# A two-layer encoder with experts: order of the router's tail, splits ahead of the routing weights, norm roots by a power on POOL

## The chip, the cores and the metric

The kernel runs on one NeuronCore of a Trainium2 chip. The metric is the device time of one launch in microseconds (us). Engines are called PE (TensorE), DVE (VectorE), ACT (ScalarE), POOL (GpSimd) and SP (SyncE, which here only issues transfers).

## The reference

Two encoder layers work on 512 tokens of width 1024 in fp32. Cut to what matters here:

```python
for layer in range(2):
    h = rms_norm(x, norm1_g[layer])
    proj = h @ w_in[layer]                      # queries, keys, values of four mixers
    y_a, y_b, y_c, y_d = mla(...), dilated(...), gqa(...), diff(...)
    mixed = concat([rms_norm(y_a), rms_norm(y_b), rms_norm(y_c), y_d]) * mix_beta[layer]
    x = x + mixed @ w_out[layer]
    x = x + hier_moe(rms_norm(x, norm2_g[layer]), ...)

def hier_moe(t, wg, bg, we, be, w_gate, w_up, w_down):
    g_w, g_idx = top_k(softmax(t @ wg + bg), 1)          # one of 4 groups
    e_logits = (t @ we + be) of that group               # 4 experts each
    e_w, e_idx = top_k(softmax(e_logits), 2);  e_w /= sum(e_w)
    gate = one_hot(expert_id) * g_w * e_w                # 512 x 16
    for e in range(16):
        y += gate[:, e] * ((silu(t @ w_gate[e]) * (t @ w_up[e])) @ w_down[e])
```

`rms_norm` is `x * rsqrt(mean(x*x) + 1e-6) * gain`. Each expert has three fp32 matrices of 2 MB.

## The kernel before, in words

Tokens stand in four row tiles of 128 (index `t`). A layer is: norm and in-projection, the four mixers as 64 units of attention (head and row tile) in a software pipeline, out-projection and router in the last steps of that pipeline, then the 16 experts. An expert gets at most 96 tokens (`CAP`); what is beyond that would be done in rounds by `overflow()`, a `tc.If` on the number of rounds. With these inputs the branch isn't taken, but every engine loads the number (`nrd`) and branches there (L1461, L1470).

Every fp32 product is made from three: an operand is split into `hi` (a rounded copy, by ACT, L144) and `lo` (the difference, by DVE or POOL, L145), and `mm3` (L268) sums hi*hi, lo*hi and hi*lo. Weights are streamed in units of 128x1024 (512 KB) by the class `Weights`: a unit is loaded into a raw buffer by SP's queue, then split into one of six pairs of `hi` and `lo` buffers, and its raw buffer is free for the next load as soon as it is split. An expert has 12 units, four each of gate, up and down, each six matmuls on PE. The experts' order on PE is expert 0's gate and up, expert 1's gate, expert 0's down, expert 1's up, expert 2's gate, and so on.

The order of the work in the last steps of attention is a table, `TAIL`: the words of step 57 to 69 are run one after the other when that step of the pipeline has been issued. A letter is a function, a digit its row tile, and G or V (or none) the engine: `r` is the norm of the tile's new stream (`norm_x`, its root is the tile `r2`), `e` turns the tile, `f` makes the router's logits (`pl` on PE, `lg` on DVE), `h` the normed rows and their write to DRAM (`h2d`), `p` the ranks of the logits and the places of the tokens (`route`: `rank`, `M`, then `pp`, `pos`, `oh`), `x` picks expert 0's rows by a one-hot matmul (`acc`), `l` lists expert 1's rows (`pli`, L1141), `s` splits the next weight unit, `T` splits expert 0's turned rows (`xh`, `xl`), `K` makes the routing weights (`weights()`: some 25 small operations on DVE, among them the casts and subtractions of L1326 and L1328), `S` gathers expert 1's rows, `O` is the overflow. Engines run their instructions in the order in which they are issued, and a DMA issued by SP waits on SP for its buffer.

In the loop over experts a `todo` table says at which unit the one-hots of a later expert are made (`listed`, DVE, `oh` L341) and at which its list is made and its rows are gathered (`start`: PE `pli` L1381, POOL's gather L1393). Two units later its rows are turned (`ptg` L1405) and split.

A narrow norm takes its root by `rstd`: an integer first guess (three operations on DVE), then three Newton rounds, on DVE (nine operations) or on POOL (twelve).

Of the kernel before, what the change touches and what calls it, by code (L numbers as in the profile page):

```python
# [62 lines left out]
def hybrid_encoder(ctx: ExitStack, tc: tile.TileContext, I: dict, out: bass.AP, depth=2, dbg=None):  # L63
# [18 lines left out]
    tokb = cst.tile([128, NT, 2], BF, name="tokb")  # L82
    wlast = cst.tile([128, NT], FT, name="wlast")
    brep = drm.tile([8, 128, 1024], FT, name="brep")

    def late_constants():
# [33 lines left out]

    def rstd(pool, ss, n, inv, name, E=V):

        x = "" if E is V else "g"
        v = pool.tile([128, n], FT, name=name + "v", tag="rsv" + x, bufs=1)
        y = pool.tile([128, n], FT, name=name + "y", tag=name + "y")
        f = pool.tile([128, n], FT, name=name + "f", tag="rsf" + x, bufs=1)
        ti = pool.tile([128, n], I32, name=name + "i", tag="rsi" + x, bufs=1)
        V.tensor_scalar(v, ss, inv, EPS, op0=OP.mult, op1=OP.add)
        V.tensor_scalar(ti, v.bitcast(I32), 1, None, op0=OP.logical_shift_right)
        V.tensor_scalar(y.bitcast(I32), ti, -1, 0x5f3759df, op0=OP.mult, op1=OP.add)  # L130
        for _ in range(3):
            if E is V:
                V.scalar_tensor_tensor(f, v, -0.5, y, op0=OP.mult, op1=OP.mult)
                V.tensor_tensor(f, f, y, op=OP.mult)
                V.scalar_tensor_tensor(y, f, 1.5, y, op0=OP.add, op1=OP.mult)
            else:
                E.tensor_tensor(f, y, y, op=OP.mult)
                E.tensor_tensor(f, f, v, op=OP.mult)
                E.tensor_scalar(f, f, -0.5, 1.5, op0=OP.mult, op1=OP.add)
                E.tensor_tensor(y, y, f, op=OP.mult)  # L140
        return y
# [181 lines left out]
    for layer in range(depth):  # L323
# [32 lines left out]
        with ExitStack() as c2:  # L356
# [425 lines left out]
            with ExitStack() as c3:  # L782
# [134 lines left out]
                def finish(mi):  # L917
# [3 lines left out]
                    if mi == 2:  # L921
                        for t in range(NT):
                            sq = sm.tile([128, 512], FT, name="sq", bufs=1)
                            A.activation(sq[:, :256], y[:, t], AF.Square, accum_out=ss_[:, t:t + 1])
                        yield LATER
                        r = rstd(sm, ss_, NT, 1.0 / 256, "yr", G)
                        for t in range(NT):
                            if t in Y2G:
                                G.tensor_tensor(y[:, t], y[:, t], r[:, t:t + 1].to_broadcast([128, 256]), op=OP.mult)
                                G.tensor_tensor(y[:, t], y[:, t], late['beta'][:, sl], op=OP.mult)  # L930
                        yield LATER
                        for t in range(NT):
                            if t not in Y2G:
                                V.scalar_tensor_tensor(y[:, t], y[:, t], r[:, t:t + 1], late['beta'][:, sl],
                                                       op0=OP.mult, op1=OP.mult)
                        for _ in range(WAIT2):
                            yield LATER
                    else:
# [5 lines left out]
                        r = rstd(sm, ss_, NT, 1.0 / 256, "yr", G)  # L944
# [13 lines left out]
                def finish_pair():  # L958
# [30 lines left out]
                def norm_pair(t, E):  # L989
                    sl, y = slice(896, 1024), Y[3][:, t, 128:]  # L990
                    r = rstd(sm, late['yss', t], 2, 1.0 / 64, "yr", E)
                    if E is V:
# [17 lines left out]
                def norm_x(t, E):  # L1010
                    V.tensor_scalar(ss2[:, t, 0:1], ss2[:, t, 0:1], ss2[:, t, 1:2], None, op0=OP.add)
                    late['r', t] = rstd(sm, ss2[:, t, 0:1], 1, 1.0 / D, "r2", E)

# [43 lines left out]
                def logits(t):  # L1057
                    pl = ps.tile([128, 512], FT, name="pl", tag="tr")[:, :20]
                    for k in range(8):
                        PE.matmul(pl, late['xT'][t % 2][:, k], late['wr'][:, k], start=k == 0, stop=k == 7)  # L1060
                    V.scalar_tensor_tensor(lg[:, t], pl, late['r', t], late['brg'][:, :20], op0=OP.mult, op1=OP.add)

# [25 lines left out]
                def route(t):  # L1088


                    l4 = lg[:, t].rearrange("p (r e) -> p r e", e=4)
# [5 lines left out]
                    for k, op in enumerate((OP.is_gt, OP.is_ge)):  # L1097
# [5 lines left out]
                    V.scalar_tensor_tensor(M[:, t].rearrange("p (g e) -> p g e", g=4), rank[:, t, 4:].rearrange("p (g e) -> p g e", g=4),  # L1103
                                           2.0, goh[:, t, :, None].to_broadcast([128, 4, 4]), op0=OP.is_lt, op1=OP.mult)
                    pp = ps.tile([128, 512], FT, name="pp", tag="tr")
                    for u in range(t + 1):
                        PE.matmul(pp[:, :NE], tri[:, 0 if u == t else 1], M[:, u], start=u == 0, stop=u == t)
# [5 lines left out]
                    V.tensor_scalar(late['oh'][:, t], iota, pos[:, t, 0:1], None, op0=OP.is_equal)  # L1113
                    if t == NT - 1:
                        oh1 = scr[:, 1536:1536 + NT * CAP // 2].bitcast(BF).rearrange("p (t c) -> p t c", t=NT)
                        late['oh1'] = hots(1, oh1)
                        count_rounds(pp[:, NE:2 * NE])

# [27 lines left out]

                STAGES = dict(l=list_rows, b=norm_pair, c=turn_pair, o=open_out, d=close_out, e=turn_x, r=norm_x, f=logits, h=normed,
                              p=route, x=pick, s=lambda E: W.split(W.done + 1, E), w=warm)
# [151 lines left out]
        with ExitStack() as c2:  # L1300
# [157 lines left out]
            def overflow():  # L1458
# [11 lines left out]
                with tc.If(rounds > 1):  # L1470
                    V.memset(off, 0.0)
                    SP.dma_start(posd[0].rearrange("(t p) e -> p t e", p=128), pos)
                    SP.dma_start(posd[1].rearrange("(t p) e -> p t e", p=128), gate)
                    with tc.For_i(1, rounds):
                        V.tensor_scalar(off, off, float(CAP), None, op0=OP.add)
                        with tc.For_i(0, NE) as e:
                            one = bass.ds(e, 1)
                            pe_ = sm.tile([128, 2, NT], FT, name="pe")
                            for j in range(2):
                                SP.dma_start(pe_[:, j], posd[j, :, one].rearrange("(t p) o -> p (t o)", p=128))  # L1480
                            V.tensor_scalar(pe_[:, 0], pe_[:, 0], off, None, op0=OP.subtract)
# [190 lines left out]
```

## Time and profile before

| what | us |
|---|---|
| three runs | 1390.12, 1398.99, 1395.04 |
| their median | 1395.04 |
| the profiled execution | 1398.48 |
| its span, first to last instruction | 1396.6 |
| mean granted clock of TensorE | 0.966 of full speed |
| PE busy | 1296.7 (93%) |
| DVE busy | 1079.7 (77%) |
| ACT busy | 876.9 (63%) |
| POOL busy | 390.9 (28%) |

The profile is of one execution; all durations below come from it. Busy times are sums over the span and say nothing of when an engine stood still. A stage is read from windows (busy time of each engine in a stretch), then from the timeline of the engine that stands still there (each row with the idle time before it and the operation that ended that idle time), and then from the timelines of the engines named.

### The profile page before, as it was taken

The numbers are of one execution on the slowest core, as the hardware profiler recorded it, in microseconds if no ns is written. First come the engines' busy times: TensorE is split into PE (matmuls) and PEld (weight loads), VectorE is DVE, ScalarE is ACT, GpSimd is POOL, SyncE is SP. The second block draws the span as 40 slices with busy tenths as digits, with TensorE's granted clock in tenths as the row PEclk, the third lists the DMA queues.
The fourth block names the chain that finished last, engine by engine and source line by source line (L and its number), as shares of the span: only waits on it lengthen the run. The fifth ranks groups of instructions, "written<-read, shape, count | busy, mean of one in ns | idle before, by whom it ended". The sixth has DMA issues, their size and how long they took to land.

```text
span 1396.6 us, 21240 instructions
## 1 busy us (share of the span) xinstructions
PE 1296.7 (93%) x7206; PEld 1024.0 (73%) x7206; DVE 1079.7 (77%) x2100; ACT 876.9 (63%) x1439; POOL 390.9 (28%) x670
## 2 busy tenths in 40 slices
PE   7999799999969999999989998999998799999996
PEld 6777688888846676666777877888886566676674
DVE  4648456879688999999876585678777799999994
ACT  3444346766347888888744444676744588888884
POOL 4205724313432111111032156332345121111120
PEclk8999879999989999999999998999999899999998
DMA  6344221011879999999444332110166899999960
GB/s 187 112 126 172 70 60 41 28 59 46 316 283 303 361 367 368 362 366 330 141 132 125 91 101 71 39 41 27 61 248 242 288 345 374 371 363 363 372 210 13
DMA packets 99935, 278.46 MB, mean 199 GB/s; under 512 B 18441, under 2 KB 29881, under 8 KB 99816
## 3 DMA queue, kind: packets, MB, share of 16 engines
q1 hardware_dynamic: 88888, 247.95, 49.8%
q0 software_dynamic: 10352, 27.41, 7.8%
q10 hardware_dynamic: 576, 1.64, 0.3%
q8 instruction: 59, 0.97, 0.3%
q14 instruction: 60, 0.49, 0.1%
HBM read 264.34 MB, written 24.81 MB: 207 GB/s over the span
## 4 chain that ended last, share of the span: by engine, by line
PE 25%; DMA 17%; DVE 14%; issue 9%; POOL 3%; ACT 3%; POOLq 0%; SPq 0%; ACTq 0%; DVEq 0%
PE pm L268 8%; DMA raw<-in_expert_w_up_dram 6%; DVE lo L145 6%; DMA raw<-in_expert_w_down_dram 5%; PE pd L268 5%; DMA raw<-in_expert_w_gate_dram 4%; PE pv L903 3%; PE ptr L276 3%; PE pu L268 2%; PE pg L268 2%; ACT hi L144 1%; DMA out_dram<-ye,ix 1%; ACT ye L1454 1%; DVE oh L341 1%; DMA x_sb<-in_expert_w_up_dram 1%
## 5 line engine op out<-in xcount | busy, mean ns | idle before, releaser
L145 DVE TENSOR_TENSOR lo<-raw,hi 128x1024 fp32r<-128x1024 f32 (+2 forms) x400 | 484.9, 1234 | 83.3 <-ACT hi L144 73.4
L144 ACT ACTIVATE hi<-raw 128x1024 fp32r<-128x1024 f32 (+1 forms) x410 | 422.5, 1050 | 93.1 <-PE pu L268 20.1
L268 PE MATMUL pm<-hi,hTh 128*128 128x512 f32 (+2 forms) x384 | 139.3, 363 | 9.5 <-DVE qkl L145 6.7
L268 PE MATMUL pm<-lo,hTh 128*128 128x512 f32 (+2 forms) x384 | 138.0, 359 | 5.4 <-DVE lo L145 5.4
L268 PE MATMUL pm<-hi,hTl 128*128 128x512 f32 (+2 forms) x384 | 138.2, 360 | 0.4
L268 PE MATMUL pg<-lo,xh 128*96 128x512 f32 x256 | 103.0, 402 | 7.1 <-POOL lo L145 4.6
L268 PE MATMUL pg<-hi,xh 128*96 128x512 f32 x256 | 104.4, 408 | 5.6 <-ACTq L1470 4.2
L268 PE MATMUL pu<-hi,xh 128*96 128x512 f32 (+1 forms) x272 | 108.9, 400 | 0.0
L268 PE MATMUL pd<-hi,hl 128*96 128x512 f32 x256 | 102.1, 399 | 4.5 <-DVE hl L145 4.5
L268 PE MATMUL pu<-lo,xh 128*96 128x512 f32 (+1 forms) x272 | 105.8, 389 | 0.0
L268 PE MATMUL pu<-hi,xl 128*96 128x512 f32 (+1 forms) x272 | 104.8, 385 | 0.0
L903 PE MATMUL pv<-v,pT 128*128 128x64 f32 x768 | 98.6, 271 | 6.5 <-DVE pT L891 2.7
L268 PE MATMUL pd<-lo,hh 128*96 128x512 f32 x256 | 101.2, 395 | 1.6 <-DVE lo L145 1.6
L903 PEld LDWEIGHTS pv<-v,pT 128*128 128x128 f32 x768 | 94.0, 193 | 10.6 <-DVE pT L891 4.7
L874 ACT ACTIVATE p<-p,m 128x512 f32<-128x512 f32 x96 | 68.7, 717 | 52.2 <-DVE m L856 51.9
L268 PE MATMUL pg<-hi,xl 128*96 128x512 f32 x256 | 101.5, 397 | 0.0
L268 PE MATMUL pd<-hi,hh 128*96 128x512 f32 x256 | 100.8, 394 | 0.0
L268 PEld LDWEIGHTS pm<-hi,hTh 128*128 128x128 f32 x384 | 75.0, 195 | 22.2 <-DVE qkl L145 7.6
L268 PEld LDWEIGHTS pm<-lo,hTh 128*128 128x128 f32 x384 | 75.0, 195 | 16.4 <-DVE lo L145 7.4
L276 PE MATMUL ptr<-ident,p 128*128 128x128 f32 x512 | 81.3, 283 | 5.8 <-ACT p L872 5.5
L276 PEld LDWEIGHTS ptr<-ident,p 128*128 128x128 f32 x512 | 67.0, 146 | 25.0 <-ACT p L872 6.4
L268 PEld LDWEIGHTS pm<-hi,hTl 128*128 128x128 f32 x384 | 75.1, 196 | 10.9 <-DVE hTl L145 2.1
(365 smaller groups left out, 2775.6 us busy)
## 6 DMA issues: line engine op xcount, KB each, us to landing
raw<-in_expert_w_down_dram SPq DMA_DIRECT2D x116, 512.0 KB
raw<-in_expert_w_gate_dram SPq DMA_DIRECT2D x114, 512.0 KB
raw<-in_expert_w_up_dram SPq DMA_DIRECT2D x112, 512.0 KB
raw<-in_w_in_dram SPq DMA_DIRECT2D x32, 512.0 KB
raw<-in_w_out_dram SPq DMA_DIRECT2D x16, 512.0 KB
toep<-brep SPq DMA_DIRECT2D x16, 448.0 KB
x_sb<-in_expert_w_gate_dram SPq DMA_DIRECT2D x14, 512.0 KB
x_sb<-in_expert_w_down_dram SPq DMA_DIRECT2D x12, 512.0 KB
```

What stands on the lines that cost most here:

```text
L144: A.activation(hi, src, AF.Copy)
L145: E.tensor_tensor(lo, src, hi.bitcast(FT), op=OP.subtract)
L268: PE.matmul(pt, a, b, start=first and n == 0, stop=last and n == tot - 1)
L276: PE.transpose(pt[:c, i * 128:(i + 1) * 128], s, ident)
L341: V.tensor_scalar(oh[:, t], iota, pos[:, t, e:e + 1], None, op0=OP.is_equal)
L874: A.activation(p, p, AF.Exp, bias=m, scale=-1.0, accum_out=s)
L903: PE.matmul(st['pv'][:, t], self.pT[:, k * 128:(k + 1) * 128], self.v(k), start=k == 0, stop=k == NT - 1)
L1454: A.activation(ye[:CAP, n * 512:(n + 1) * 512], self.pd[n], AF.Copy, scale=self.w)
```

## The change

Five things are changed, in both layers.

1. A root of at most eight columns (all but one kind) is two operations on POOL: `tensor_scalar` for mean plus epsilon, `tensor_tensor` with `pow` and a constant tile of -0.5.
2. Steps 67 to 69 of `TAIL` are reordered. `f` is parted into `f` (matmuls) and `g` (`lg`), `p` into `p` (ranks), `P` (places) and `N` (the list's one-hots and the number of rounds). Units are split on DVE (`sV`) twice in 67, once in 68 and three times in 69, there right behind `T` and ahead of `K`; POOL's splits of 69 are gone. The gather of expert 1 (`S`) stands ahead of the overflow.
3. The overflow's transfers are issued by ACT in place of SP.
4. A table `FIRST` sets at which units experts 2, 3 and 4 are listed and started.
5. The lists of expert 0 and 1 (for their gates) move from expert 0's up units to their own down units.

```diff
-        67: "f0 b3G o2 p0 r1V f1 h1 d2 o3 r2G e2 x0 p1 c3 d3 f2 e3 h30 x1 r3G p2 h2 f3",
-        68: "x2 h31 p3 l x3",
-        69: "T K m sG B O q sG S"}
+        67: "f0 g0 b3G o2 p0 P0 r1V f1 g1 h1 d2 o3 r2G e2 sV x0 p1 P1 h2 c3 d3 r3G h30 f2 g2 e3 p2 f3 P2 g3 sV x1 p3 P3 x2 h31",
+        68: "x3 N l sV",
+        69: "T sV sV sV m S K B O q"}
...
+FIRST = ((2, ((0, 'u', 1), (0, 'u', 3))), (3, ((1, 'g', 1), (1, 'g', 3))), (4, ((1, 'u', 0), (1, 'u', 2))))
...
+    G.memset(mhalf, -0.5)
...
-    def rstd(pool, ss, n, inv, name, E=V):
+    def rstd(pool, ss, n, inv, name):
+
+        few = n <= 8
+        x = "g" if few else ""
...
+        if few:
+            G.tensor_scalar(v, ss, inv, EPS, op0=OP.mult, op1=OP.add)
+            G.tensor_tensor(y, v, mhalf.to_broadcast([128, n]), op=OP.pow)
+            return y
...
-            if E is V:
-                V.scalar_tensor_tensor(f, v, -0.5, y, op0=OP.mult, op1=OP.mult)
-                V.tensor_tensor(f, f, y, op=OP.mult)
-                V.scalar_tensor_tensor(y, f, 1.5, y, op0=OP.add, op1=OP.mult)
-            else:
-                E.tensor_tensor(f, y, y, op=OP.mult)
-                E.tensor_tensor(f, f, v, op=OP.mult)
-                E.tensor_scalar(f, f, -0.5, 1.5, op0=OP.mult, op1=OP.add)
-                E.tensor_tensor(y, y, f, op=OP.mult)
+            V.scalar_tensor_tensor(f, v, -0.5, y, op0=OP.mult, op1=OP.mult)
+            V.tensor_tensor(f, f, y, op=OP.mult)
+            V.scalar_tensor_tensor(y, f, 1.5, y, op0=OP.add, op1=OP.mult)
...
-                    SP.dma_start(r, w)
+                    A.dma_start(r, w)
...
-                    SP.dma_start(posd[0].rearrange("(t p) e -> p t e", p=128), pos)
-                    SP.dma_start(posd[1].rearrange("(t p) e -> p t e", p=128), gate)
+                    A.dma_start(posd[0].rearrange("(t p) e -> p t e", p=128), pos)
+                    A.dma_start(posd[1].rearrange("(t p) e -> p t e", p=128), gate)
...
-                    for s, todo in ((e + 3, (('u', 0), ('u', 2))),) + (((2, (('g', 2), ('u', 0))),) if e == 0 else ()):
-                        if (m, i) in todo and s < NE:
-                            (start if (m, i) == todo[1] else listed)(s)
-                    if (e, m) == (0, 'u') and i in (0, 2):
-                        j = i // 2
-                        X[j].hots = hots(j, sm.tile([128, NT, CAP], BF, name="oh", bufs=2))
-                        X[j].lists(lambda t: parts[:, t, j], rows=j == 0)
+
+                    for s, todo in FIRST if e < 2 else ((e + 3, (('u', 0), ('u', 2))),):
+                        if e > 1:
+                            todo = [(e,) + w for w in todo]
+                        if (e, m, i) in todo and s < NE:
+                            (start if (e, m, i) == todo[1] else listed)(s)
+                    if m == 'd' and e < 2:
+                        if i == 0:
+                            X[e].hots = hots(e, sm.tile([128, NT, CAP], BF, name="oh", bufs=2))
+                        elif i == 2:
+                            X[e].lists(lambda t: parts[:, t, e], rows=e == 0)
```

What this does to the order on the engines is seen at three places, each before and then in the changed kernel.

First DVE where the experts begin: `xl` are expert 0's split rows, `mxg` to `parts` the routing weights, `oh` the one-hots of the lists. Before:

```order
L145 TENSOR_TENSOR xl<-acc,xh 128x384 x2
L1333 TENSOR_REDUCE mxg<-lg 128x4
...
L1326 CAST parts<-first 128x64
L1461 TENSOR_LOAD nrd
L1470 COMPARE_AND_BRANCH
...
L1470 UNCONDITIONAL_BRANCH
L145 TENSOR_TENSOR lo<-raw,hi 128x1024 x5
L341 TENSOR_SCALAR oh<-iota,pos 128x96 x4
L145 TENSOR_TENSOR lo<-raw,hi 128x1024 x2
L341 TENSOR_SCALAR oh<-iota,pos 128x96 x4
```

In the changed kernel:

```order
L147 TENSOR_TENSOR lo<-raw,hi 128x1024
L147 TENSOR_TENSOR xl<-acc,xh 128x384 x2
L147 TENSOR_TENSOR lo<-raw,hi 128x1024 x2
L1344 TENSOR_REDUCE mxg<-lg 128x4
...
L1337 CAST parts<-first 128x64
L1472 TENSOR_LOAD nrd
L1481 COMPARE_AND_BRANCH
...
L1481 UNCONDITIONAL_BRANCH
L147 TENSOR_TENSOR lo<-raw,hi 128x1024 x5
L147 TENSOR_TENSOR xl<-ptg,xh 128x384 x2
L343 TENSOR_SCALAR oh<-iota,pos 128x96 x4
```

Three splits (and two more among the router's operations) now stand ahead of the branch, and behind it expert 1's turned rows come before the first one-hots.

Then SP from the loads of the third gate to the overflow's branch (`nrd` is the number of rounds). Before:

```order
L186 DMA x_sb<-in_expert_w_gate_dram 128x1024 x2
L186 DMA raw<-in_expert_w_gate_dram 128x1024
L183 DMA raw<-in_expert_w_down_dram 128x1024 x4
L186 DMA raw<-in_expert_w_up_dram 128x1024 x2
L1461 TENSOR_LOAD nrd
```

In the changed kernel:

```order
L188 DMA x_sb<-in_expert_w_gate_dram 128x1024 x2
L188 DMA raw<-in_expert_w_gate_dram 128x1024
L185 DMA raw<-in_expert_w_down_dram 128x1024 x4
L188 DMA raw<-in_expert_w_up_dram 128x1024 x4
L188 DMA raw<-in_expert_w_gate_dram 128x1024
L188 DMA x_sb<-in_expert_w_gate_dram 128x1024
L188 DMA raw<-in_expert_w_gate_dram 128x1024
L1472 TENSOR_LOAD nrd
```

Behind the pair to `x_sb` SP issues 12 loads ahead of the branch in place of 7; one of the further five was ACT's before (`x_sb<-in_expert_w_up_dram`, issued in `weights()`). SP keeps its wait for the semaphores of all loads at the branch's end in both.

Last ACT behind the branch: `sg` is the silu of expert 0, `xh` are expert 1's turned rows. Before:

```order
L1470 UNCONDITIONAL_BRANCH
L144 ACT_TABLE_LOAD
L144 ACTIVATE hi<-raw 128x1024 x7
L1419 ACT_TABLE_LOAD
L1419 ACTIVATE sg<-pg 96x512
L144 ACTIVATE hi<-raw 128x1024 x2
L144 ACTIVATE xh<-ptg 128x384 x2
```

In the changed kernel:

```order
L1481 UNCONDITIONAL_BRANCH
L146 ACT_TABLE_LOAD
L146 ACTIVATE hi<-raw 128x1024 x3
L1430 ACT_TABLE_LOAD
L1430 ACTIVATE sg<-pg 96x512
L146 ACTIVATE hi<-raw 128x1024 x2
L146 ACTIVATE xh<-ptg 128x384 x2
```

Four of the `hi` copies moved ahead of the branch; the silu's table load waits for the semaphores of all loads in both kernels, since its tile `sg` is also the target of the overflow's loads.

## Rows read from the trace of the kernel before

**Rows 1.** Windows of before: us, each engine's busy time (instructions), PEclk, DMA share, GB/s.

```profile
345.00:391.00 46.00, 43.75 (x289) 37.91 (x288) 32.00 (x114) 15.42 (x41) 23.67 (x74) 1.00 0.72 270
400.00:410.00 10.00, 7.36 (x23) 4.17 (x23) 8.76 (x8) 7.50 (x8) 4.85 (x5) 0.83 0.74 270
```

**Rows 2.** Timeline of before, PE: start us, us, line, operation, count, [idle before <-releaser].

```profile
394.59 0.45 PE L268 MATMUL pg<-hi,xh 128*96 128x512 f32 x1 [0.78 <-PEq L1470]
...
409.10 0.40 PE L268 MATMUL pu<-lo,xh 128*96 128x512 f32 x1
...
409.33 0.39 PE L268 MATMUL pu<-hi,xl 128*96 128x512 f32 x1
...
415.69 0.78 PE L1381 MATMUL pli<-parts,oh 128*96 128x5 bf16 x4 [3.27 <-DVE oh L341]
...
416.85 0.63 PE L268 MATMUL pu<-lo,xh 128*96 128x512 f32 x1
...
417.27 0.63 PE L268 MATMUL pu<-hi,xl 128*96 128x512 f32 x1
...
426.84 0.63 PE L268 MATMUL pg<-hi,xh 128*96 128x512 f32 x1
...
433.24 0.40 PE L268 MATMUL pd<-hi,hh 128*96 128x512 f32 x1
```

**Rows 3.** Source line L1470 of before: duration ns min/median/max, first and last start us.

```profile
L1470 SPq EVENT_SEMAPHORE  x16: 17/17/17, 407.7 to 1087.7; - x16
L1470 PEldq EVENT_SEMAPHORE  x2: 51/51/51, 394.5 to 1073.6; - x2
```

**Rows 4.** Chain of waits of before, layer 1: start us, us, what.

```profile
1112.39 2.77 PE pd L268 x12
```

**Rows 5.** Timeline of before, DVE.

```profile
387.92 0.24 DVE L1061 SCALAR_TENSOR_TENSOR lg<-pl,r2y,br 128x20 f32<-128x20 f32 x1 [0.64 <-POOL r2y L140]
...
394.85 0.16 DVE L1333 TENSOR_REDUCE mxg<-lg 128x4 f32<-128x16 f32 x1
...
398.50 2.20 DVE L1328 TENSOR_TENSOR first<-gate,parts 128x64 f32<-128x64 f32 x1
...
400.74 3.17 DVE L1326 CAST parts<-first 128x64 bf16<-128x64 f32 x1
...
404.26 0.26 DVE L1326 CAST parts<-first 128x64 bf16<-128x64 f32 x1
...
405.66 5.77 DVE L145 TENSOR_TENSOR lo<-raw,hi 128x1024 fp32r<-128x1024 f32 x5 [1.14 <-DVEq L1470]
...
411.35 0.81 DVE L341 TENSOR_SCALAR oh<-iota,pos 128x96 bf16<-128x96 f32 x4
```

**Rows 6.** Timeline of before, POOL.

```profile
383.73 0.20 POOL L137 TENSOR_TENSOR r2f<-r2y 128x1 f32<-128x1 f32 x1 [0.50 <-DVE r2y L130]
...
387.69 0.19 POOL L140 TENSOR_TENSOR r2y<-r2y,r2f 128x1 f32<-128x1 f32 x1
...
398.26 2.35 POOL L145 TENSOR_TENSOR lo<-raw,hi 128x1024 fp32r<-128x1024 f32 x1 [7.22 <-ACTq L1470]
...
401.39 2.39 POOL L145 TENSOR_TENSOR lo<-raw,hi 128x1024 fp32r<-128x1024 f32 x1
```

**Rows 7.** Timeline of before, ACT.

```profile
408.93 1.28 ACT L1419 ACT_TABLE_LOAD   x1 [2.47 <-SPq L1470]
...
410.72 1.99 ACT L144 ACTIVATE hi<-raw 128x1024 fp32r<-128x1024 f32 x2
...
419.86 1.13 ACT L144 ACTIVATE xh<-ptg 128x384 fp32r<-128x384 f32 x2 [7.15 <-PE ptg L1405]
```

**Rows 8.** Windows of before, columns as in group 1.

```profile
388.20:407.70 19.50, 11.29 (x59) 7.45 (x58) 16.03 (x47) 11.65 (x15) 9.18 (x9) 0.91 0.92 337
395.00:400.00 5.00, 1.67 (x7) 0.69 (x5) 4.59 (x21) 3.19 (x5) 1.74 (x1) 1.00 1.03 407
```

**Rows 9.** Lines of before, POOL, shapes apart: count | busy us, mean ns | idle, releaser.

```profile
L592 POOL TENSOR_TENSOR h<-x_sb,lo 128x1024 f32<-128x1024 f32 x3 | 7.8, 2627 | 24.4 <-DVE x_sb L1595 24.4
```

More of the change, by code (lines that the diff above doesn't have):

```diff
@@ L83, in hybrid_encoder @@
     wlast = cst.tile([128, NT], FT, name="wlast")
+    mhalf = cst.tile([128, 1], FT, name="mhalf")
     brep = drm.tile([8, 128, 1024], FT, name="brep")
+    G.memset(mhalf, -0.5)
     def late_constants():
@@ L118, in bias_steps @@
             SP.dma_start(brep, btd[:, None, :].to_broadcast([8, 128, 1024]))
-    def rstd(pool, ss, n, inv, name, E=V):
-        x = "" if E is V else "g"
+    def rstd(pool, ss, n, inv, name):
+        few = n <= 8
+        x = "g" if few else ""
         v = pool.tile([128, n], FT, name=name + "v", tag="rsv" + x, bufs=1)
         y = pool.tile([128, n], FT, name=name + "y", tag=name + "y")
-        f = pool.tile([128, n], FT, name=name + "f", tag="rsf" + x, bufs=1)
-        ti = pool.tile([128, n], I32, name=name + "i", tag="rsi" + x, bufs=1)
+        if few:
+            G.tensor_scalar(v, ss, inv, EPS, op0=OP.mult, op1=OP.add)
+            G.tensor_tensor(y, v, mhalf.to_broadcast([128, n]), op=OP.pow)
+            return y
+        f = pool.tile([128, n], FT, name=name + "f", tag="rsf", bufs=1)
+        ti = pool.tile([128, n], I32, name=name + "i", tag="rsi", bufs=1)
         V.tensor_scalar(v, ss, inv, EPS, op0=OP.mult, op1=OP.add)
@@ L925, in finish @@
                         yield LATER
-                        r = rstd(sm, ss_, NT, 1.0 / 256, "yr", G)
+                        r = rstd(sm, ss_, NT, 1.0 / 256, "yr")
                         for t in range(NT):
@@ L943, in finish @@
                             V.tensor_reduce(ss_[:, t:t + 2], sq, axis=AX.X, op=OP.add)
-                        r = rstd(sm, ss_, NT, 1.0 / 256, "yr", G)
+                        r = rstd(sm, ss_, NT, 1.0 / 256, "yr")
                         yield LATER
@@ L967, in finish_pair @@
                     V.tensor_reduce(ss_, sq, axis=AX.X, op=OP.add)
-                    r = rstd(sm, ss_.rearrange("p t h -> p (t h)"), NT * 2, 1.0 / 64, "yr", G)
+                    r = rstd(sm, ss_.rearrange("p t h -> p (t h)"), NT * 2, 1.0 / 64, "yr")
                     rv = r.rearrange("p (t h) -> p t h", t=NT)
@@ L990, in norm_pair @@
                     sl, y = slice(896, 1024), Y[3][:, t, 128:]
-                    r = rstd(sm, late['yss', t], 2, 1.0 / 64, "yr", E)
+                    r = rstd(sm, late['yss', t], 2, 1.0 / 64, "yr")
                     if E is V:
@@ L1011, in norm_x @@
                     V.tensor_scalar(ss2[:, t, 0:1], ss2[:, t, 0:1], ss2[:, t, 1:2], None, op0=OP.add)
-                    late['r', t] = rstd(sm, ss2[:, t, 0:1], 1, 1.0 / D, "r2", E)
+                    late['r', t] = rstd(sm, ss2[:, t, 0:1], 1, 1.0 / D, "r2")
                 def sq2():
@@ L1060, in logits, with logged @@
                         PE.matmul(pl, late['xT'][t % 2][:, k], late['wr'][:, k], start=k == 0, stop=k == 7)
-                    V.scalar_tensor_tensor(lg[:, t], pl, late['r', t], late['brg'][:, :20], op0=OP.mult, op1=OP.add)
+                    late['pl', t] = pl
+                def logged(t):
+                    V.scalar_tensor_tensor(lg[:, t], late['pl', t], late['r', t], late['brg'][:, :20], op0=OP.mult, op1=OP.add)
                 def normed(t, part=None):
@@ L1104, in route, with places @@
                                            2.0, goh[:, t, :, None].to_broadcast([128, 4, 4]), op0=OP.is_lt, op1=OP.mult)
+                def places(t):
+                    scr = late['scr']
                     pp = ps.tile([128, 512], FT, name="pp", tag="tr")
+                    late['pp'] = pp
                     for u in range(t + 1):
@@ L1113, in route, with next_list @@
                     V.tensor_scalar(late['oh'][:, t], iota, pos[:, t, 0:1], None, op0=OP.is_equal)
[L1114 to L1117, printed above, removed]
+                def next_list():
+                    oh1 = late['scr'][:, 1536:1536 + NT * CAP // 2].bitcast(BF).rearrange("p (t c) -> p t c", t=NT)
+                    late['oh1'] = hots(1, oh1)
+                    count_rounds(late['pp'][:, NE:2 * NE])
                 def count_rounds(cnt):
@@ L1145, in list_rows @@
                     X[1] = bass.IndirectOffsetOnAxis(ap=ix[:CAP], axis=0)
-                STAGES = dict(l=list_rows, b=norm_pair, c=turn_pair, o=open_out, d=close_out, e=turn_x, r=norm_x, f=logits, h=normed,
+                STAGES = dict(l=list_rows, g=logged, P=places, N=next_list, b=norm_pair, c=turn_pair, o=open_out, d=close_out, e=turn_x, r=norm_x, f=logits, h=normed,
                               p=route, x=pick, s=lambda E: W.split(W.done + 1, E), w=warm)
@@ L1479, in overflow @@
                             for j in range(2):
-                                SP.dma_start(pe_[:, j], posd[j, :, one].rearrange("(t p) o -> p (t o)", p=128))
+                                A.dma_start(pe_[:, j], posd[j, :, one].rearrange("(t p) o -> p (t o)", p=128))
                             V.tensor_scalar(pe_[:, 0], pe_[:, 0], off, None, op0=OP.subtract)
```

## The prediction

> **What bounds the kernel now.** The windows come first [rows 1]: read the PE column and the granted clock. Through the last stretch of the out-projection and the router (345 to 391 us) PE works 43.75 of 46 us. Then, in 400 to 410, it falls to 7.36 of 10 us at clock 0.83. So what can be won in bulk lies between the end of the router and the first down-projection. The PE timeline sizes it [rows 2]. I number the experts' weight units in the order PE takes them: expert 0's gate u0 to u3, its up u4 to u7, expert 1's gate u8 to u11, then the first down unit u12. PE leaves the branch of the overflow code and starts u0 at 394.59, and starts u12 (`pd`) at 433.24: 38.7 us for 12 units. The reader should see the cadence from 409.10 to 409.33, 0.23 us a matmul, against 0.42 between 416.85 and 417.27 (the lower of the two clocks, 1.2 against 2.4 GHz, after an idle stretch). 72 matmuls at 0.23 are 16.6 us, so about 20 us are lost. In layer 1 PE leaves the branch at 1073.6 [rows 3] and starts `pd` at 1112.39 [rows 4]: 38.8 us, the same loss. About 40 us is thus the most this change can touch there.
>
> Next, who makes PE wait. On DVE [rows 5] the weights chain stands between the router and the next units, from 394.85 on. One of its casts took 3.17 us and the subtraction ahead of it 2.20, beside POOL's splits [rows 6]; the cast's twin took 0.26. Five `lo` splits follow only at 405.66, then the one-hots of the lists at 411.35, for which PE waits until 415.69 [rows 2]. On ACT [rows 7] the silu's table load at 408.93 waited 2.47 us, put down to SP's branch; behind the silu stand two `hi` copies and then `xh`, expert 1's turned rows. SP explains that [rows 3]: leaving the untaken branch, it is free at 407.7 (1087.7 in layer 1), because its loads have to land first. From 388.2 to 407.7 the 16 DMA engines moved 337 GB/s at a busy share of 0.92 [rows 8].
>
> **The change, part by part.**
>
> *Splits.* Five `lo` move ahead of the branch on DVE (u1 to u5), none stays on POOL, where u1 and u2 were. Five at 5.77/5 = 1.15 us [rows 5]. u0 to u5 can then run without waits: 36 matmuls, 8.3 us. On DVE u3 stands ahead of `xl`, which would delay u0 by 1.15 us; `acc` no longer waits for the list's matmuls, about as much earlier. I take u0 where it was, so u5 ends near 403. u4 and u5 take DVE to about 398.6, the weights chain (9.7 us from 394.85, less 2.9 on the cast and 1.9 on the subtraction) 4.9 us, the branch 1.1: `lo` of u6 and u7 end near 406 and 407, and PE has u7 done at 408.2. Before, u7 ended at 426.84. This part alone would give 18 us a layer.
>
> *What is late next.* u8 needs `xh` of expert 1, and ACT still has the silu, `hi` and `hi` ahead of it. The silu still waits for SP's join: in the changed kernel's list of instructions SP keeps its wait for all eight load semaphores at the branch's end, and the silu's table load keeps its own, although the overflow's loads are now ACT's. And SP issues more before it gets there: 12 loads instead of 7 follow the third router tile's logits, one of them formerly ACT's, so four more in sum, 2.1 MB. Before, 337 GB/s for 19.5 us is 6.57 MB [rows 8]; now 8.67 MB. At 337 GB/s that is 25.7 us. At 407 GB/s, as in 395 to 400, it is 21.3, and about 1.3 until the first bytes: 22.6. I take the middle, 24. The loads start when `lg` of the last tile ends, 388.16 before [rows 5]. `lg` waits for the root `r2`, whose three Newton rounds took POOL from 383.73 to 387.88 [rows 6]. With a short root it waits for its matmuls instead, which move up by the 2 us of `acc` now behind them: about 386.7. So the join comes near **410.7** instead of 407.7.
>
> From there: table load and silu 1.79 (408.93 to 410.72), two `hi` 1.99, `xh` 1.13 [rows 7], `lo` and `xl` still due on DVE about 0.9, four one-hots 0.81 [rows 5], their list on PE 0.78 [rows 2]: 7.4 us, u8 at 418.1 (before 426.84). PE has idled since 408.2, longer than before 415.69, so I charge it again the lower clock that the rows show there: eleven matmuls 0.2 us slower, 2.2. u8 to u11 24 x 0.23 = 5.5, a list and four transposes 1.1: `pd` at 426.9, **6.3** us earlier. Layer 1 has the same rows about 679 us later: 6.3 again. Sum 12.6.
>
> *A rule on queues.* A DMA share of 1.03 in 395 to 400 [rows 8], with loads of SP and ACT under way, leaves no room that another queue could open. The Trainium skill, "DMA: Bandwidth & Descriptors", section "Issuing engines are not separate DMA queues", says that transfers started by any engine run on the same 16 DMA engines and that another queue saves only the issue time. By it the load that goes from ACT to SP adds no traffic (four more, as above); were the queues separate, five would come on top of SP's, 2.6 MB, and the join 1.4 us later. The share speaks for the rule.
>
> *Narrow roots on POOL.* Fifteen a layer become two POOL operations: ten had 3 DVE and 12 POOL operations, five had 12 on DVE. No `pow` stands in this trace. Bounds: 0.19 us, POOL's last round of `r2` [rows 6], and 2.63 us, POOL's longest computation on any tile [rows 9]. I take 0.3, nearest to the rows of equal width. At 2.63 `r2` is still ready sooner than after its old 4.2 us. Elsewhere PE hides it: in 345 to 391 it idles 2.25 us in all [rows 1], the most to win there, and nothing is lost unless POOL fills up (below). I take 0.75 a layer, **1.5** in sum.
>
> *Overflow on ACT's queue.* The branch isn't taken, so nothing is issued; ACT jumps further. DVE passed the same jump in 1.14 us [rows 5]; 0 to 1 us more on ACT ends before the join. *FIRST.* Experts 2 to 4 are listed later, expert 0's and 1's own lists move to their down units: of 12 one-hots between the splits four are left before u8, counted above. *Gather of expert 1* goes ahead of the branch and lands before `xh` asks for it.
>
> Sum 12.6 + 1.5 = 14.1 against the profiled execution's own 1398.48: 1384.4. That execution lies 3.4 above the median of the runs, 1395.04, so I forecast **1381**.
>
> **Rivals.**
> 1. *The join does not bind.* If the loads land by about 404, the silu runs beside u4 to u7, PE never idles long, u8 starts near 410 and `pd` near 416.5: 16.7 us a layer, with the roots 35 in all, 1360. For it: u1's and u2's raw buffers are released earlier, by DVE. Against it: 8.67 MB from 386.7 would need 500 GB/s, above any row. Only fewer loads ahead of the join, or a silu that no longer waits, would do it. Chance 0.17.
> 2. *The join moves out further.* At 414 some 3 us a layer are left, at 417 nothing: 1388 to 1395. For it: loads are issued in order, and the last now waits for a split that ends at 398.6; 270 GB/s were moved in 400 to 410 [rows 1], at which 8.67 MB take 32 us. Chance 0.20.
> 3. *Slower: POOL fills up with roots.* In 345 to 391 POOL works 23.7 us [rows 1], six to seven Newton chains of it (4.2 less its gaps, some 2.6 to 3 each), 18 in sum at most. Without them 6 to 8 stay, and about seven new roots stand in that stretch, so a `pow` of 5.5 us fills it. Above that each further us holds up `lg`, and everything behind it, by 7 us a layer. To lose 14 us beyond the 14 won takes 14 a layer, about 7.5 us a root: 1409 or more. Against it: nothing POOL computes here took over 2.63 [rows 9]. Chance 0.08.
> 4. *The splits don't move*, for want of free buffers. The list of instructions excludes it: they stand ahead of the branch.
>
> **How the numbers follow.** The forecast's own case has 0.55. Its bounds, a join 1.4 us earlier or 1.7 later and 0 to 2.25 a layer for the roots, give 1376 to 1386; with the spread of the runs 1374 to 1388. About 1% (14 us) is what a measurement of this kernel can tell from no change, so the border of faster lies at 1381.1, in the middle of that case: 0.30 of it falls below, 0.25 above. With rival 1 faster has 0.47, same 0.25 + 0.20 = 0.45, slower 0.08. The range for 8 in 10 takes in most of rivals 1 and 2: 1362 to 1394.
>
> **What would show it.** In the changed profile: no POOL `lo` and no half-clock rows in the first six units; SP's join near 410.7 and 1090 (near 404: rival 1; behind 414: rival 2); the silu's table load released by SP; `pd` 32.3 us after the branch; roots of two POOL rows, 0.2 to 0.4 each. A wrong forecast most likely comes from the join's time, which counts one to one, twice.

## The result, and the profile after

The changed kernel takes **1405.70 us** in the median (1400.78 to 1410.36) against 1395.43 for the kernel before on the same chip: ratio 1.0064, 95% interval 1.0049 to 1.0079. It is slower by some 10 us, where 1381 was forecast. The profiled execution has 1403.28 us, a span of 1401.5 and a mean granted clock of 0.956 (before 1398.48, 1396.6, 0.966).

First PE's timeline of the changed kernel, layer 0 [rows 2], and two rows of `acc` of the kernel before.

```profile
369.20 1.92 PE L1145 MATMUL acc<-scr,h 128*128 128x96 f32 x16
...
373.74 0.17 PE L1116 MATMUL pp<-M,tri 128*128 128x16 bf16 x1 [2.60 <-DVE M L1107]
...
384.48 0.17 PE L1116 MATMUL pp<-M,tri 128*128 128x16 bf16 x1 [0.98 <-DVE M L1107]
384.50 3.71 PE L1145 MATMUL acc<-scr,h 128*128 128x96 f32 x16
...
388.26 6.87 PE L1145 MATMUL acc<-scr,h 128*128 128x96 f32 x32
...
395.42 0.44 PE L270 MATMUL pg<-hi,xh 128*96 128x512 f32 x1
...
407.87 0.74 PE L270 MATMUL pu<-hi,xh 128*96 128x512 f32 x1 [5.22 <-ACTq L1481]
...
415.72 0.39 PE L270 MATMUL pu<-hi,xl 128*96 128x512 f32 x1
...
424.03 0.78 PE L1392 MATMUL pli<-parts,oh 128*96 128x5 bf16 x4 [7.92 <-DVE oh L343]
...
432.71 0.45 PE L270 MATMUL pd<-hi,hh 128*96 128x512 f32 x1
```

```profile
375.92 1.92 PE L1134 MATMUL acc<-scr,h 128*128 128x96 f32 x16
...
391.81 2.00 PE L1134 MATMUL acc<-scr,h 128*128 128x96 f32 x16
```

Three things are new: PE waits for `M` twice in the router's tail, `acc` then takes twice its time for 48 matmuls (10.6 us, the 1.2 GHz clock; `PEclk` is 0.50 to 0.52 there), and u7, done at 416.1, is followed by 7.92 us of nothing. `pd` starts at 432.71, 0.5 us earlier than before, but only because this execution reached its first `acc` 6.7 us earlier (369.20 for 375.92): from there to `pd` it takes 63.5 us for 57.3. In layer 1 `pd` starts at 1115.66 for 1112.23, 63.0 us behind the first `acc` for 57.1. The source rows of the branch say why u8 is late [rows 3].

```profile
L1481 SPq EVENT_SEMAPHORE  x16: 17/17/17, 408.1 to 1100.7; - x16
...
L1481 ACTq COMPARE_BRANCH  x2: 45/48/50, 402.3 to 1085.1; - x2
...
L1481 ACTq EVENT_SEMAPHORE  x2: 17/17/17, 407.8 to 1085.6; - x2
```

SP's join ends at 1100.7 in layer 1 (1087.7 before) and near 417.6 in layer 0, as ACT's silu shows [rows 7]:

```profile
407.94 1.28 ACT L146 ACT_TABLE_LOAD   x1 [5.95 <-ACTq L1481]
...
417.64 1.28 ACT L1430 ACT_TABLE_LOAD   x1 [5.46 <-SPq L1481]
```

SP's queue, 386 to 420 us (waited for: us, times, longest), names what held the loads up: the first row is the wait ahead of their start, the second one stands between them. Then DVE's timeline of that stretch [rows 5].

```profile
SPq L188 <- DVE scr L1102: 15.8, 1, 15.8
...
SPq L185 <- DVE lo L147: 9.9, 1, 9.9
```

```profile
381.78 1.18 DVE L1106 TENSOR_SCALAR goh<-rank 128x4 f32<-128x4 f32 x1
382.99 1.43 DVE L1107 SCALAR_TENSOR_TENSOR M<-rank,goh 128x16 bf16<-128x16 f32 x1
...
385.08 0.23 DVE L1066 SCALAR_TENSOR_TENSOR lg<-pl,r2y,br 128x20 f32<-128x20 f32 x1
...
395.31 0.16 DVE L1154 TENSOR_REDUCE scr<-pli 96x1 f32<-96x2 f32 x1 [4.92 <-PE pli L1152]
...
395.57 1.23 DVE L147 TENSOR_TENSOR lo<-raw,hi 128x1024 fp32r<-128x1024 f32 x1
396.72 1.01 DVE L147 TENSOR_TENSOR xl<-acc,xh 128x384 fp32r<-128x384 f32 x2
397.65 2.44 DVE L147 TENSOR_TENSOR lo<-raw,hi 128x1024 fp32r<-128x1024 f32 x2
```

The split of u3 stands behind the reduction of expert 1's list; that waits 4.92 us for `pli`; `pli` now stands on PE behind all of `acc`. Only when the split ends (396.8) is a raw buffer free for SP's next load. The windows show the hole [rows 1, 8]:

```profile
390.00:400.00 10.00, 8.61 (x44) 7.33 (x44) 4.98 (x10) 2.87 (x4) 2.31 (x3) 0.76 0.22 66
400.00:410.00 10.00, 4.78 (x17) 3.06 (x16) 4.22 (x25) 2.47 (x4) 0.00 (x0) 0.75 1.00 371
...
386.50:417.60 31.10, 23.00 (x109) 17.90 (x107) 15.41 (x51) 7.53 (x10) 2.84 (x4) 0.76 0.67 246
```

Last POOL's timeline [rows 6], where `h` is tile 3's half of the normed rows, and the new roots by width (count | busy us, mean ns | idle).

```profile
380.86 0.60 POOL L132 TENSOR_TENSOR r2y<-r2v,mhalf 128x1 f32<-128x1 f32 x1
381.44 2.95 POOL L1085 TENSOR_TENSOR h<-x_sb,hi 128x512 f32<-128x512 f32 x2
```

```profile
L132 POOL TENSOR_TENSOR yry<-yrv,mhalf 128x4 f32<-128x4 f32 x6 | 6.1, 1014 | 0.5
...
L132 POOL TENSOR_TENSOR r2y<-r2v,mhalf 128x1 f32<-128x1 f32 x8 | 4.6, 572 | 0.7
...
L132 POOL TENSOR_TENSOR yry<-yrv,mhalf 128x8 f32<-128x8 f32 x2 | 3.3, 1662 | 0.2
```

### The profile page after: what moved, and what is told of

Same layout as the page of the kernel before. It is cut to its first block, busy times and chain, and to the rows that moved or that the text cites. A ratio compares the mean times of both kernels' runs of the same rounds, so it can differ in the third digit from the quotient of the medians.

```text
span 1401.5 us, 20877 instructions
## 1 busy us (share of the span) xinstructions
PE 1294.8 (92%) x7206; PEld 1026.3 (73%) x7206; DVE 1046.8 (75%) x1924; ACT 876.5 (63%) x1439; POOL 373.9 (27%) x487
## 5 line engine op out<-in xcount | busy, mean ns | idle before, releaser
L147 DVE TENSOR_TENSOR lo<-raw,hi 128x1024 fp32r<-128x1024 f32 (+1 forms) x404 | 489.9, 1234 | 112.1 <-ACT hi L146 100.1
```

What stands on the lines that cost most here:

```text
L147: E.tensor_tensor(lo, src, hi.bitcast(FT), op=OP.subtract)
```

## The experiments

The theory: the loss is the join, 7 us (layer 0) and 10.7 us (layer 1) later than forecast by the clocks of the two executions, and the join is late because SP's loads stand still behind the split of u3; the silu passes it on because its tile is also a target of the overflow's loads. Rivals: ACT's longer jump, POOL's roots, and PE's half clock in the router.

Single executions lie up to 8 us off the median of their kernel (E1's profiled one by 8.0 below it), so the traces are compared by a stretch inside of them: from the first `acc` to the first `pd` (before 375.92 to 433.24, after 369.20 to 432.71).

| kernel | median us | ratio to before, 95% | stretch, layer 0 / 1 |
|---|---|---|---|
| before | 1395.43 | | 57.3 / 57.1 |
| after | 1405.70 | 1.0064 [1.0049, 1.0079] | 63.5 / 63.0 |
| E1 after, silu free | 1391.53 | 0.9971 [0.9957, 0.9985] | 54.2 / 52.2 |
| E2 before, silu free | 1396.76 | 1.0002 [0.9979, 1.0025] | 58.9 / 57.1 |
| E3 before, new roots | 1394.94 | 0.9991 [0.9970, 1.0012] | 57.6 / 56.6 |
| E4 after, overflow on SP | 1407.06 | 1.0075 [1.0055, 1.0095] | 62.6 / 63.2 |
| E5 after, u3 split first | 1396.31 | 0.9997 [0.9980, 1.0014] | 58.3 / 56.4 |
| E6 after, router order | 1400.21 | 1.0029 [1.0010, 1.0047] | 59.6 / 62.2 |
| E7 after, rows ahead of root | 1403.86 | 1.0054 [1.0034, 1.0074] | 60.6 / 60.4 |
| E8 after, all mended | 1377.41 | 0.9872 [0.9853, 0.9891] | 46.8 / 46.7 |
| E9 E8, order without waits | 1373.57 | 0.9849 [0.9825, 0.9874] | 44.8 / 45.1 |
| E10 E8, overflow on ACT | 1382.31 | 0.9904 [0.9882, 0.9925] | 53.1 / 46.7 |
| E11 E9, x1 between logits | 1372.07 | 0.9828 [0.9798, 0.9857] | 43.8 / 45.4 |
| E12 E11, x2 ahead of P3 | 1373.40 | 0.9841 [0.9808, 0.9873] | 45.6 / 45.3 |

**E1 and E2, the silu freed from the join** (in the changed kernel and in the kernel before).

```diff
-                    r = sm.tile([128, 512], FT, name="sg", bufs=1)
+                    r = xg[0][:, :512]
```

> The changed kernel, but the weights that the overflow would load go to the last row tile of the stream in place of the silu's tile sg, so that the silu no longer waits for SP's join. If the join is what holds expert 1's gate back (main theory): silu at about 412 in place of 417.6 in layer 0 and 1090 in place of 1100.9 in layer 1, u8 as much earlier, less half clock, 15 to 20 us in all: about 1387 where the changed kernel took 1405.7, faster than before by 0.5%. If the late splits or the clock in the router's tail are the cause instead: within 3 us of 1405.7.

> The kernel before with the same other target for the overflow's weights. In its trace PE's last gate matmul ended at 408.3, just ahead of the silu, and PE then waited for one-hots on DVE: main theory 0 to 2 us, that is no difference. If the join bound it too: 5 us faster or more.

E1 is 13 to 14 us faster than the changed kernel (by the ratios and by the medians; 15 to 20 were expected), E2 is no different from the kernel before. ACT's timeline of E1, then PE's:

```profile
402.71 1.28 ACT L146 ACT_TABLE_LOAD   x1 [5.80 <-ACTq L1481]
...
406.97 1.28 ACT L1430 ACT_TABLE_LOAD   x1
```

```profile
402.65 0.47 PE L270 MATMUL pu<-hi,xh 128*96 128x512 f32 x1 [3.51 <-ACTq L1481]
...
413.36 0.78 PE L1392 MATMUL pli<-parts,oh 128*96 128x5 bf16 x4 [2.68 <-DVE oh L343]
...
421.42 0.45 PE L270 MATMUL pd<-hi,hh 128*96 128x512 f32 x1
```

The silu's table load waits for nobody and the wait ahead of u8 goes from 7.92 to 2.68 us. So the join was the binding wait in the changed kernel, and the earlier splits are worth something once it is gone. In the kernel before the join was nearly hidden by the late splits. ACT's jump, hidden until then, now costs PE 3.51 us ahead of u4 in layer 0.

**E3, the new roots alone**, in the kernel before: only `rstd` and its constant tile are those of the change.

> The kernel before with the roots on POOL by pow and nothing else. In the trace after, such a root takes 0.19 + 0.60 us; the last r2 took 4.9 before. Main theory: lg of the last tile 3 us earlier in each layer and some 2 us from attention in layer 0: 5 to 8 us faster, about 1389. If the roots are what made the change slow: slower than before by up to 9 us.

No difference was measured: the interval runs from 4.2 us faster to 1.7 us slower, so the 5 to 8 us expected here did not come, while the 1.5 us of the forecast are neither shown nor excluded. DVE's and POOL's rows of E3, tile 3, show a part of what took the gain back:

```profile
385.19 1.50 DVE L1103 TENSOR_SCALAR goh<-rank 128x4 f32<-128x4 f32 x1
386.73 0.18 DVE L1104 SCALAR_TENSOR_TENSOR M<-rank,goh 128x16 bf16<-128x16 f32 x1
```

```profile
385.18 0.53 POOL L1085 DMA_DIRECT2D h2d<-h  x1
385.70 0.97 POOL L1525 MEMSET xg<- 128x1024 f32 x1
```

`lg` comes 0.6 us sooner after the first `acc` (11.4 us for 12.0). But POOL, free earlier, runs its next work beside the ranks: `goh` takes 1.50 us (0.17 before) and ends with POOL's memset, and PE waits 1.32 us for `M` (0.56 before). The last `acc` takes 3.71 us for 2.00 in layer 0, but that can't be laid to the roots: E2, without them and with a wait of 0.57 us, has the same 3.71.

**E4, the overflow's transfers back on SP** in the changed kernel (`A.dma_start` to `SP.dma_start`, four lines).

> The changed kernel with the overflow's transfers back on SP's queue. In the trace after ACT stood 5.5 us in the jump over the branch in layer 0 (0.5 in layer 1). Main theory: that jump goes, but the silu waits for SP's join all the same, so 0 to 2 us faster than the changed kernel, about 1404. If the jump is the main loss: 5 us or more faster, 1400.

No difference from the changed kernel (0 to 2 us faster were expected); its rows of the branch, beside those of after above, give the jump's price:

```profile
L1481 ACTq COMPARE_BRANCH  x2: 45/45/45, 403.9 to 1088.8; - x2
...
L1481 ACTq EVENT_SEMAPHORE  x2: 17/17/17, 404.4 to 1089.2; - x2
```

It is 0.5 us here in both layers; with the larger body it is 5.5 us in layer 0 and 0.5 in layer 1. Behind the join it costs nothing.

**E5, u3's split ahead of the list.**

```diff
-        68: "x3 N l sV",
+        68: "sV x3 N l",
```

> The changed kernel with one word moved: in step 68 the split of the next unit (u3) stands ahead of x3, N and l, so that DVE frees its raw buffer before it waits for expert 1's list (pli) on PE. Theory: half of what went wrong is SP's 9.9 us behind that buffer. SP then goes on near 391.5 in place of 396.8, the join lies near 412.5 (1095.5 in layer 1) in place of 417.6 and 1100.7, pd follows it, 5 us a layer earlier: about 1396, ratio to the kernel before 1.000. Rival: the next loads then wait for the splits of u4 and u5, which still stand behind the list and xl (ends 398.9 and 400.1), so that the join moves by under 2 us: 1403 or more.

1396.31, as the theory said. The 9.9 us are gone; of SP's waits between the loads (386 to 415 us) these are the longest:

```profile
SPq L185 <- DVE scr L343: 3.6, 1, 3.6
SPq L188 <- PE acc L1145: 2.0, 1, 2.0
```

From `lg` of the last tile to the silu's release it takes 26.9 and 25.4 us (32.6 in both layers of the changed kernel, 21.0 and 20.7 before, 24 forecast to the join). One word in the order holds nearly all of the loss against the kernel before, and with it in place the forecast's loading time is nearly met. `lg` of tile 3 itself still comes 15.5 and 15.8 us behind the first `acc`, as in the changed kernel (15.9 and 15.6) and not as before (12.0 in both layers).

**E6 and E7, the router's order:** E6 moves both places, E7 only h30.

```diff
-  ... r2G e2 sV x0 p1 P1 h2 c3 d3 r3G h30 f2 g2 ...
+  ... r2G e2 x0 p1 P1 sV h2 c3 d3 h30 r3G f2 g2 ...
```

> The changed kernel with two places in step 67 as a waiting PE would like them: the first split stands behind x0, p1 and P1 in place of ahead of them, and POOL's half of tile 3's normed rows (h30) stands ahead of r3G, as in the kernel before. Theory: both wrong places make PE wait for M (2.6 and 1.0 us), after which its matmuls run at the lower clock; without them the 48 matmuls of acc take about 6 us in place of 10.6, pli and with it u3's split and SP's loads come 4 to 6 us earlier, and the join and pd follow by about 4 a layer: 1398, ratio 1.002. Rival: the clock and u0 return to 391, but the join is set by the amount of loads and stays within 1 us, PE only idles longer in front of u8: 1405 or more.

> The changed kernel with one of the two places of the router order alone: h30 ahead of r3G. It tells whether the DVE operations that took 1.18 and 1.43 us in place of 0.17 (goh and M of tile 2) were stretched by POOL's 2.95 us beside them. Theory: they return to 0.17 each or stand clear of POOL, PE's wait for that M goes from 0.98 to under 0.5 and acc runs at the full clock; but r3 then stands behind h30 on POOL and lg of tile 3 comes up to 1 us later. About half of the router order's gain: 1401 to 1403. Rival: the stretch comes from something else (DVE's own queue) and stays, and nothing moves: 1406.

E6 came near in time and failed in its reason. The waits for `M` are gone, but PE waits 1.93 us for DVE's `m` (behind the split and `h2`), and `acc` still takes 3.71 and 6.28 us. In E7 `goh` and `M` are back at 0.17 us each, clear of POOL's `h`, PE's second wait for `M` is 0.62 us and `acc` takes 2.74 and 5.85 us. Its time, a little above the 1401 to 1403 expected, isn't told apart from the changed kernel's. Of E6's gain (5.5 us by the medians) the traces show 3.9 us in layer 0's stretch, 2.9 of them a sooner `lg` of tile 3 (13.0 us behind the first `acc` for 15.9); layer 1's stretch is 0.8 us shorter, and there `lg` comes 0.9 us later (16.4 for 15.6).

**E8, all mended:** the edits of E1, E4, E5 and E6 in the changed kernel.

> The changed kernel with all that was found wrong put right: the overflow's weights land in the idle raw rows of expert 0 and no longer in the silu's tile, its transfers are issued by SP again, the split of u3 stands ahead of the list, and the router order is that of the run beside it. Theory: the silu waits for nothing, ACT jumps in 0.5 us, acc takes 6 us, u0 starts near 391 and u0 to u11 run with one short wait for the list: pd near 413 (421.4 with the silu freed alone) and 1088. Layer gain about 8 each over that run, 1391.5: 1375 to 1378, ratio 0.986. Rival: with the silu free the bound is the arrival of the weights themselves (u8 and its followers come in at about 350 GB/s), so that an earlier u0 only waits later, and the time stays at 1388 to 1391.

1377.41: faster than both kernels, within the theory's range, though not by its way: u0 starts 22.8 us behind the first `acc` (26.2 after, 18.7 before), since `acc` still runs at the half clock. PE of E8:

```profile
403.01 0.58 PE L270 MATMUL pu<-hi,xh 128*96 128x512 f32 x1 [3.29 <-DVEq L1481]
...
417.67 0.45 PE L270 MATMUL pd<-hi,hh 128*96 128x512 f32 x1
```

In layer 0 only this wait of 3.29 us ahead of u4 is left between u0 and `pd`. u4 was split in time; but its `pu` takes a PSUM buffer that the overflow's body uses too (tag `pv` in both places of the code), so PE waits until DVE has left the branch behind the routing weights. A kernel without this sharing wasn't tried.

**E9, the order without waits.**

```diff
-  ... x0 p1 P1 sV h2 c3 d3 h30 r3G f2 g2 e3 p2 f3 P2 g3 sV x1 p3 P3 x2 h31
+  ... x0 p1 P1 c3 h2 d3 h30 r3G f2 g2 e3 p2 sV f3 P2 g3 x1 p3 P3 sV x2 h31
```

> As the version with all mended, but with step 67 ordered by what DVE is asked for: tile 3's turned columns (c3) right behind P1, then h2; the first split in the gap in which DVE waited 1.16 us for pp of tile 2, the second behind P3 in place of ahead of the ranks of tile 3. In the version with all mended PE still waited 1.93 us for DVE's m (behind that split and h2) and its clock still fell to one half some 7 us later, for acc (3.71 and 6.85 us). Theory: the halved clock follows any idle stretch of some 2 to 4 us in the out-projection's end; without one acc's 48 matmuls take about 6 us in place of 10.6, lg of tile 3 and SP's loads come 1.5 to 2 us earlier, u0 starts near 388.5 in place of 393.65; of that the loads let only 2 to 3 us a layer through to pd: 1372 to 1374. Rival: the first split, 8 us later, frees its buffer later, the loads start no earlier, and the time stays at 1376 to 1378.

The time is in the theory's range, though its interval overlaps E8's. Half of the reason holds: `lg` of tile 3 comes 11.3 us behind the first `acc`, 12.4 and 13.0 in E8. The half on the clock falls. PE of E9, layer 0, without an idle stretch over 0.2 us:

```profile
378.51 1.86 PE L1062 MATMUL pl<-wr,lo 128*128 128x20 f32 x16
380.21 1.14 PE L278 MATMUL ptr<-ident,x_sb 128*128 128x128 f32 x8
381.54 1.96 PE L1062 MATMUL pl<-wr,xT 128*128 128x20 f32 x16 [0.18 <-ACT xT L1057]
...
383.74 3.65 PE L1145 MATMUL acc<-scr,h 128*128 128x96 f32 x16
```

Before the fall PE ran 5.2 us of narrow matmuls (logits, turns, ranks) with no wait over 0.2 us. In the kernel before the same rows have 16 of `acc` in their middle.

**E10, E8 with the overflow on ACT.**

> The version with all mended, but with the overflow's transfers on ACT's queue again, as in the changed kernel. Theory: ACT's jump over the untaken body takes 5.5 us in layer 0 and 0.5 in layer 1, and with the silu free of the join it is no longer hidden in layer 0: u4's hi copies and the silu come 3 to 4 us later there, 1380 to 1381. Rival: the copies wait for the up weights until about 400 anyway and the jump costs nothing: 1377.

1382.31, a little above the range: ratio 0.9904 against 0.9872, 4.5 us, with intervals that just overlap. u4's `hi` copy, which the expectation names, was not what waited (it stands ahead of the branch), but the trace has the place: layer 0's stretch is 53.1 for 46.8 us, and layer 1 is the same to 0.1. PE waits 5.38 us ahead of u4 for ACT to leave the branch (3.29 for DVE in E8); the silu, with expert 1's `xh` behind it, comes 5.1 us later behind u0, and PE waits 2.37 us more ahead of u8's list, where E8 has no wait.

**E11 and E12, x1 between the logits; then also x2 and h31 ahead of P3.**

```diff
-  ... e3 p2 sV f3 P2 g3 x1 p3 P3 sV x2 h31
+  ... e3 x1 p2 sV f3 P2 g3 p3 P3 sV x2 h31
```

> As the version ordered without waits, with one word moved: x1 (acc of tile 1, 16 matmuls of 96 columns) stands ahead of p2 and f3, between tile 2's and tile 3's logits, as in the kernel before. In the version without waits PE never stood still over 0.2 us from 373 to 394, and its clock fell to one half at 383.7 all the same, after 5.2 us of narrow matmuls (logits of 20 columns, turns of 128, ranks of 16). Theory: that narrow stretch and not a wait halves the clock; with x1 in it acc takes 1.9 us per tile at the full clock, u0 starts near 391 in place of 394.67, layer 1 likewise, and 2 us a layer reach pd: 1370. Rival: the clock is halved by what lies earlier or at random, acc stays at 10.6 us for the three tiles and the time at 1373.6.

> As the version with x1 between the logits, and x2 and h31 ahead of P3, so that PE picks tile 2's rows while DVE ranks tile 3 and doesn't wait for M. Theory: PE stands still nowhere, x2 hides the wait for M of tile 3 of about 1 us and u0 starts near 390; what is late next is then the routing weights on DVE and the up weights' arrival near 400, so that at most 1 us a layer more is won: 1368 to 1370. Rival: the loads bind, 1370 or no change against the version with x1 alone.

PE of E11:

```profile
379.01 1.92 PE L1145 MATMUL acc<-scr,h 128*128 128x96 f32 x16
...
385.09 0.17 PE L1116 MATMUL pp<-M,tri 128*128 128x16 bf16 x1 [1.87 <-DVE M L1107]
...
385.21 5.42 PE L1145 MATMUL acc<-scr,h 128*128 128x96 f32 x32
```

x1 runs at the full clock again, but it now stands where in E9 too the clock hadn't fallen yet (378.5 to 383.7), so this alone doesn't show the theory. The three tiles take 7.3 us for 10.6; PE then waits 1.87 us for `M`, and part of the last 32 runs slow. In E12 x2 waits 1.81 us for DVE instead and takes 3.73 us: E12 misses its range; "no change", which its rival laid to the loads, is what was measured. E9, E11 and E12 are not told apart in time (1372 to 1374, 0.983 to 0.985 of the kernel before). What exactly lowers the clock stays open: rows show it low after waits of 0.98 to 2.60 us and, in E9, after narrow work without such a wait. Nor does the order alone settle it: E1 has the changed kernel's order up to there, and in its layer 0 the last 32 of `acc` take 3.79 us, at the full clock, for 6.87.

## Why the prediction was wrong

- **The failed step is the join's time:** "The loads start when `lg` of the last tile ends", 24 us, "so the join comes near 410.7". It came at 417.6 and 1100.7 for 410.7 and 1090. The larger part is the 24 us: the loads were priced as one unbroken flow of 8.67 MB. They moved 7.65 MB (246 GB/s for 31.1 us) with a hole of 66 GB/s from 390 to 400, and from the end of `lg` to the silu's release it took 32.3 and 32.4 us. A load needs a buffer that a split frees. I counted the split of u3 as ready early and not as queued on DVE behind a wait for PE's last `acc`. E5 shows this: one word took back 9.4 of the 24.7 us between forecast and result (1405.70 for 1381). Besides, 407.7, the time before, was the first of SP's eight waits in layer 0 and not the last (the silu left at 408.9), 1.2 us of the miss.
- **The start of the loads** was right only by luck (SP issued at 386.5 for 386.7): this execution was 6.7 us ahead at the first `acc`, where the executions of the changed kernel and of E1 and E4 to E12 lie anywhere from 367.2 to 377.3. Counted from the first `acc`, `lg` of tile 3 was forecast some 1.5 us sooner than the 12.0 before and came at 15.9 and 15.6, some 5 us late in each layer. Inside that time PE waits 2.60 us for `M`, its next matmuls run at the half clock (0.63 us for 0.39), and DVE's `goh` and `M` take 1.18 and 1.43 us ahead of `lg`. The forecast put the new order in the router's tail at a gain of 2 us and looked for no wait in it. In E9, with the words reordered, `lg` comes at 11.3. So counted, the join is 13.7 and 13.3 us late.
- **From the join on** the sum was nearly right: 7.0 us to u8 in both layers (424.67 and 1107.88) for 7.4, then 8.0 and 7.8 to `pd` for 8.8. The join's error went through to `pd` almost whole: counted from the first `acc`, `pd` is 12.5 and 12.2 us behind the forecast.
- **Rival 2**, "the join moves out further", named the cause ("the last now waits for a split") with 0.20, but its price ended at no change, with a join at 417. By the trace's own time layer 0 is just beyond that; counted from the first `acc` the join lies 48.4 us behind it, which on the clock of the kernel before is 424.4. Rival 1's condition, "a silu that no longer waits", is E1: 1391.5 and not its 1360, since ACT's jump, the list and the slow `acc` were the next to bind. Rival 3 did not happen: POOL works 13.7 us in 345 to 391, for 23.7 before.
- **u0 to u5 without waits at the full clock:** u0 started at 395.42 for 394.6, which is the same luck: counted from the first `acc` it came at 26.2 us for 18.7, 4.6 of it by `acc`, which takes 10.6 us for 6.0. u4 did not run without a wait: PE stood 5.22 us until ACT had left the branch (1.26 until DVE had, in layer 1), by the shared buffer of `pu`. I had looked at the splits alone. u7 ended at 416.1 for 408.2.
- **ACT's jump** was bounded at 0 to 1 us; it took 5.5 in layer 0. That it hides behind the join was right (E4); without the join it costs some 4.5 us (E10).
- **Roots:** taken at 0.3 us, measured 0.57 to 1.66 by width. Whether the 0.75 us a layer came E3 can't tell: its interval holds 1.5 us in sum as well as nothing.
- **The weights chain** without POOL's splits took 4.7 us (400.02 to 404.74) for 4.9.
- **Left out:** from `pd` on each layer takes some 1.7 us longer (layer 0 up to its last store 263.0 for 261.3), with lists that stood ahead of `pd` now behind it. `FIRST` and that move were costed at nothing, and were not run alone, so that the cause of these 1.7 us is not shown.
- **The rule on queues** was not put to a test: with the branch untaken no transfer of the overflow runs, and E4 and E10 show only ACT's jump.

## What to carry to other kernels

When a split or copy is moved, ask not only who waits for its result but whose buffer it frees, and what it then stands behind on its engine: a wait on one engine's queue can stop another engine's loads. A wait that seems hidden has a price as soon as its cover is taken away, so look for tiles shared between a hot path and a body that never runs, and for what leaves that body last. A repair that brings nothing alone can still be needed: by the medians against the changed kernel E1 brought 14.2 us, E5 9.4, E6 5.5 and E4 none, together 28 (E8), close to their sum; but without E4's the others lose some 4.5 again (E10). And compare two traces from a common mark inside them: by absolute times the start of the loads here looked as forecast, and counted from the first `acc` it was 5 us late.

## What the runs showed of the hardware that was not expected

- A `pow` on POOL takes 0.57 us on 128x1 (`r2`; 0.91 in the two `r0`), 1.01 on 128x4 and 1.66 on 128x8: a base and about 0.16 us a column, against 0.19 for a multiplication of 128x1.
- DVE's `goh` (128x4, one input) took 1.18 and 1.50 us for 0.17 beside POOL, and ended with POOL's operation, a memset in E3. In the kernel before a cast beside POOL took 3.17 us for 0.26.
- ACT's jump over an untaken body: 5.5 us in layer 0 with the body that holds its transfers, 0.5 us in layer 1 and with the smaller body. During the 5.5 us (402.2 to 407.9) the changed kernel's trace has one packet on the instruction queue, in layer 1's 0.5 us none:

```profile
q14 instruction: 1, 0.01, 0.3%
```

The Trainium skill, "Runtime: NRT & Kernel Launch", section "Instruction fetch mechanics", says that a jump to code outside the window already loaded has to wait for a DMA to bring it. These rows are in line with that, but don't show whose code the packet brought; the price is theirs, at a busy share of the DMA engines of 1.00 (400 to 410 above).
